# Weight splits behind the router's lists, a second last tile routed alone, and final norms without GpSimd

## The chip, the cores and the metric

The kernel runs on one core of a Trainium2 chip. A core has five engines with their own instruction queues: TensorE (PE, with weight loads as PEld), VectorE (DVE), ScalarE (ACT), GpSimd (POOL) and SyncE (SP, which issues most transfers); a queue is worked off in order, and engines wait for one another by semaphores. The metric is the device time of one launch in microseconds (us). All times below come from one profiled execution unless it is said otherwise.

## What is computed

One layer of a decoder trunk on 1024 tokens of width 1024 with 16 learned tokens ahead of them: three mixers fed by one projection, their output projected and added to the stream `h`, then a mixture of 16 experts, then a final norm. The change touches the mixture and the norm:

```python
h = h + mixed @ w_out[l]
h = h + hier_moe(rms_norm(h, norm_ffn_g[l]), router_g_w[l], router_g_b[l],
                 router_e_w[l], router_e_b[l], exp_w1[l], exp_w3[l], exp_w2[l])
return rms_norm(h, final_norm_g)[:, N_META:]
```

`hier_moe` picks for each token the best of four groups (`lg`) and in it the two best of four experts, with gates from two softmaxes; an expert is `(silu(t @ w1) * (t @ w3)) @ w2`, times its gate.

## The kernel before

**Precision.** Every large product is made of three: both factors are split into a high part (rounded) and a low part (the rest). A split of half a weight buffer (128x1024) is a copy on ScalarE (L1273) and a subtraction (L1274) on VectorE, or for some of the first weights on GpSimd. A transposed token block is split the same way when it leaves PSUM (L1201 on ScalarE, L1202 on VectorE).

**Router.** The stream is worked off in eight tiles of 128 tokens. For each, `mix` multiplies by `w_out` and adds (L867), and `logits` transposes (L878), multiplies by the router's matrix (L884), takes a root mean square (`rsqrt_mean`: two short GpSimd instructions, L271 and L273) and scales the logits (L887). The normed tile goes to DRAM (`t_d`) and the stream too (`h_d`), by SP's queue. For tile 7 the norm is a scaling on ScalarE (L893) and a product with the norm's weights on GpSimd (L894). `Router.batch(a, b)` turns the logits of tiles a to b-1 into chosen experts, counts and gates: some 40 short VectorE instructions, a few small matmuls (L1052 counts), and for each tile one-hot matrices (L1066, L1068) that PE multiplies (L1071) to lists. It is called for tiles 0 to 3, 4 and 5, and, behind the last logits, for 6 and 7. `finish` reads the lists from PSUM (L1090, L1092). The gates are written to `t_d` beside the rows (L1084).

**Experts.** `moe` is a generator: its first part, up to the first `yield`, loads three raw weights, and more is set up as the stream's tiles are done. Behind the lists, GpSimd gathers an expert's tokens from `t_d` by an indirect transfer (`gather`, L1185), block 0 always and block 1 (a second 128 tokens) only if the expert has more than 128; `come` transposes them. Then follows, in an order written by hand (`ORDER`), a round for each of 16 experts: f0 and f1 the first product of block 0 and 1, g the gate function, u and v its transpose (L1221) and split (L1227), s00, s01, s1 the second product, e00 to e11 the eviction with the token's gate (L1434 for the last three experts), t and x the next expert's transposes, a0, a1, w0, w1, b0, b1 the splits of weights two or fewer experts ahead, ga the gather. The results of the first thirteen experts are added to `h_d` by scattered transfers; for the last four the kernel gathers the rows of `h_d` into SBUF ahead (L1361), adds into them and writes the normed rows to the output (`result`, L1368).

**Final norm.** A row block of 128x1024 is squared and summed on ScalarE (L1320), its root taken by L271 and L273, and scaled by the mean and the weights: one VectorE instruction (L1330), or, for the rows that `ASIDE` names, a scaling on ScalarE (L1327) and a product on GpSimd (L1328). Rows of tokens that no late expert touches are normed in rounds 14 and 15, then those of experts 12 and 13; their steps lie in the list `later`, from which `tick(n)` takes n steps at each place of the order, n from `TICKS`.

## Time and profile before

| | |
|---|---|
| runs of the kernel | 878.46, 884.48, 885.94 us; median 884.48 |
| profiled execution | 882.01 us; span from first to last instruction 880.3 us |
| mean granted TensorE clock | 0.954 of full speed |
| busy share of the span | PE 89%, VectorE 68%, ScalarE 50%, GpSimd 31% |
| mix of tile 7 to the first expert matmul | about 563 to 595 us |
| expert loop | about 595 to 858 us |
| last norms and result writes | about 858 to 880 us |

Times are positions in the profiled execution. A row of the timeline gives start, duration, engine, line and operation, output and inputs with shapes, and how many instructions it groups (x2 means two, with one duration for both). In brackets stands how long the engine had been idle before, and what ended that: another engine's instruction, a transfer (DMA), or "issue" where the profile shows no reason. PE's own end times are modelled.

### The profile page before, as it was taken

To read this page: it belongs to the slowest core of one execution; us is meant where nothing else is said; L and a number is where in the kernel's file an instruction comes from. 1 tells how busy PE (TensorE), PEld (TensorE's weight loads), DVE (VectorE), ACT (ScalarE), POOL (GpSimd) and SP (SyncE) were. 2 spreads that over 40 slices of the span, in tenths; PEclk is the share of its full clock that TensorE was granted. 3 is DMA by queue.
4 is the path that set the end of the run, shared out by engine and by line. 5 is a ranking of instruction groups with operands and counts; after the bars stand their busy time and mean duration, and the time that the engine had idled before them with its cause. 6 is when DMAs were issued, how large, how long until landed. Compare 5 with 4: busy or idle time off the path is not lost. (4 is left out here: it accounts for less than half of the span.)

```text
span 880.3 us, 13055 instructions
## 1 busy us (share of the span) xinstructions
PE 781.9 (89%) x4402; PEld 635.6 (72%) x4403; DVE 594.7 (68%) x1292; ACT 438.4 (50%) x762; POOL 274.0 (31%) x371
## 2 busy tenths in 40 slices
PE   3999999789999989999999999827999998997880
PEld 2899998678999956555668888716788885775660
DVE  5961889977644476656534345756779677897993
ACT  7222645343323375555663231415568567686861
POOL 4499948720001000000020020341223223124374
PEclk9998999999999999999999999957999999998985
DMA  8307132031320141202232422129699979899752
GB/s 275 83 7 145 50 96 61 8 98 37 98 71 13 51 139 51 73 25 73 97 101 73 142 94 77 48 88 374 230 292 285 284 227 275 273 271 291 252 208 105
DMA packets 88987, 122.00 MB, mean 139 GB/s; under 512 B 14827, under 2 KB 69898, under 8 KB 88912
## 3 DMA queue, kind: packets, MB, share of 16 engines
q1 hardware_dynamic: 81856, 101.98, 36.2%
q0 software_dynamic: 7056, 19.09, 8.0%
q8 instruction: 39, 0.64, 0.3%
q14 instruction: 36, 0.29, 0.1%
HBM read 101.16 MB, written 26.52 MB: 145 GB/s over the span
## 5 line engine op out<-in xcount | busy, mean ns | idle before, releaser
L282 PE MATMUL psum<-arena,arena 128*128 128x512 f32 (+4 forms) x848 | 306.4, 362 | 10.9 <-DVE arena L597 7.2
L283 PE MATMUL psum<-arena,arena 128*128 128x512 f32 (+4 forms) x848 | 299.9, 354 | 0.1
L284 PE MATMUL psum<-arena,arena 128*128 128x512 f32 (+4 forms) x848 | 299.5, 354 | 0.0
L282 PEld LDWEIGHTS psum<-arena,arena 128*128 128x128 f32 x848 | 162.1, 192 | 32.1 <-DVE arena L597 8.1
L284 PEld LDWEIGHTS psum<-arena,arena 128*128 128x128 f32 x848 | 162.0, 191 | 17.0 <-DVE arena L592 0.3
L283 PEld LDWEIGHTS psum<-arena,arena 128*128 128x128 f32 x848 | 162.3, 191 | 15.4 <-issue 0.4
L1274 DVE TENSOR_TENSOR arena<-arena,arena 128x1024 fp32r<-128x1024 f32 x92 | 114.3, 1278 | 18.2 <-ACT arena L1273 16.7
L1273 ACT ACTIVATE arena<-arena 128x1024 fp32r<-128x1024 f32 x96 | 98.8, 1073 | 7.9 <-DMA arena<-in_exp_w_dram 4.7
L671 DVE CUSTOM_DVE_ANT_0 arena<-psum,arena 128x144 bf16<-128x144 f32 (+6 forms) x112 | 55.1, 506 | 46.8 <-PE psum L669 24.2
L271 POOL TENSOR_SCALAR arena<-arena 128x1 f32<-128x1 f32 (+3 forms) x35 | 13.4, 383 | 231.6 <-DVE arena L463 73.0
L729 PE MATMUL psum<-arena 128*65 128x512 f32 (+4 forms) x224 | 82.8, 455 | 0.5 <-ACT arena L726 0.5
L726 ACT ACTIVATE arena<-psum,arena 128x512 f32<-128x512 f32 (+4 forms) x112 | 59.3, 539 | 47.7 <-PE psum L723 30.8
L1238 POOL DMA_INDIRECT h_d<-arena x17 | 33.6, 1979 | 127.2 <-DVE arena L1202 64.1
L1195 PE MATMUL psum<-arena 128*128 128x128 f32 x256 | 39.7, 290 | 20.8 <-DMA arena<-t_d,arena 12.7
L1201 ACT ACTIVATE arena<-psum 128x512 fp32r<-128x512 f32 x64 | 38.6, 604 | 34.2 <-PE psum L1195 34.2
L1195 PEld LDWEIGHTS psum<-arena 128*128 128x128 f32 x256 | 31.8, 149 | 32.2 <-DVE arena L1202 9.0
L430 DVE SCALAR_TENSOR_TENSOR psum<-arena,psum 128x1024 f32<-128x1024 f32 x40 | 51.4, 1285 | 0.8
L666 PE MATMUL psum<-arena 128*128 128x144 f32 (+6 forms) x112 | 51.5, 483 | 0.0
L1202 DVE TENSOR_TENSOR arena<-psum,arena 128x512 fp32r<-128x512 f32 x64 | 43.6, 683 | 11.6 <-ACT arena L1201 11.6
L718 PE MATMUL psum<-arena 128*128 128x512 f32 (+4 forms) x112 | 47.8, 427 | 2.8 <-ACT arena L726 2.5
L440 POOL TENSOR_TENSOR arena<-arena 128x512 f32<-128x512 f32 x36 | 48.1, 1359 | 1.0 <-ACT arena L437 1.0
L437 ACT ACTIVATE arena<-arena 128x512 f32<-128x512 f32 x40 | 28.3, 720 | 35.2 <-POOL arena L440 21.0
(297 smaller groups left out, 1257.5 us busy)
## 6 DMA issues: line engine op xcount, KB each, us to landing
arena<-in_exp_w_dram SPq DMA_DIRECT2D x64, 512.0 KB
arena<-in_exp_w_dram SPq DMA_DIRECT2D x16, 1024.0 KB
arena<-in_x_dram SPq DMA_DIRECT2D x16, 512.0 KB
arena<-in_w_in_dram SPq DMA_DIRECT2D x14, 512.0 KB
arena<-cr_d SPq DMA_DIRECT2D x8, 520.0 KB
arena<-in_w_out_dram SPq DMA_DIRECT2D x8, 512.0 KB
h_d<-arena SPq DMA_DIRECT2D x8, 512.0 KB
t_d<-arena SPq DMA_DIRECT2D x8, 512.0 KB
```

The costliest lines, as they stand in the source:

```text
L282: PE.matmul(out=acc, lhsT=lh[k], rhs=rh[k], start=(k == 0), stop=False)
L283: PE.matmul(out=acc, lhsT=lh[k], rhs=rl[k], start=False, stop=False)
L284: PE.matmul(out=acc, lhsT=ll[k], rhs=rh[k], start=False, stop=(k == n - 1))
L430: V.scalar_tensor_tensor(out=yc, in0=ub[:, m, w:w + NX], scalar=cwt[:, m, w:w + 1], in1=yc, op0=OP.mult, op1=OP.add)
L440: G.tensor_tensor(out=yp[:, a:a + 512], in0=yp[:, a:a + 512], in1=o, op=OP.add)
L666: PE.matmul(out=sp, lhsT=QS[:, i * 128 - 128:i * 128], rhs=KS[:, a:b], start=True, stop=not last)
L671: V.tensor_tensor_reduce(out=jk_b()[:, :b - a], in0=sp, in1=nrow[:, a:b], scale=1.0, scalar=-3.0e38, op0=OP.add, op1=OP.max, accum_out=mp[ ...
L726: S.activation(out=pt, in_=sp, func=AF.Exp, bias=ccol[:nk, j, h:h + 1])
L729: PE.matmul(out=po[:, q0 - 512 * g:512], lhsT=vt[:nk, j, h, :], rhs=pt, start=j == 0, stop=j == last, skip_group_check=True)
L1195: PE.transpose(tp[:, k, :], xg[:, c:c + 128], ident)
L1273: S.activation(out=h[:, cs], in_=raw[:, cs], func=AF.Copy)
L1274: eng.tensor_tensor(out=l[:, cs], in0=raw[:, cs], in1=h[:, cs].bitcast(F32), op=OP.subtract)
```

## The change

Line numbers of the changed kernel are higher by some 14 in `moe` (L1274 becomes L1288, L1330 becomes L1338, L1434 becomes L1442, L1185 becomes L1199).

- `logits`: for tile 7 the GpSimd product `h2 * fg_row` comes ahead of the logits (L873) and the ScalarE scaling last (L894).
- `batch` is called for tile 6 behind `logits(6)` and for tile 7 alone behind `logits(7)`. The gates become a method of their own; for tile 7 `finish` calls it last.
- `moe`: the six half splits of the first three weights move from ahead of the lists (two weights on GpSimd, one on VectorE) to behind the first gathers, all on VectorE, each weight with its refill; three further weights are loaded ahead of the lists; two of the four token buffers are cleared later; `come(1)` stands behind the first product.
- the last norms: no row on ScalarE and GpSimd any more; the steps taken at each place are counted anew; the round behind the last expert is written out by hand, the two rows of expert 14 in one norm, those of expert 15 singly.

```diff
@@ logits
+        t = t_b()
+        if i == 7:
+            G.tensor_tensor(out=t, in0=h2[i], in1=fg_row, op=OP.mult)
...
-        t = t_b()
...
-            S.activation(out=t, in_=h2[i], func=AF.Copy, scale=r1)
-            G.tensor_tensor(out=t, in0=t, in1=fg_row, op=OP.mult)
+
+            with at_priority(400):
+                S.activation(out=t, in_=t, func=AF.Copy, scale=r1)
@@ the tiles
-        if i in (4, 5):
-            rt.batch(*{4: (0, 4), 5: (4, 6)}[i])
+        if i in (4, 5, 6):
+            rt.batch(*{4: (0, 4), 5: (4, 6), 6: (6, 7)}[i])
...
-    rt.batch(6, 8)
+    rt.batch(7, 8)
@@ Router.batch and finish
+        if b < 8:
+            self.gates(a, b)
+
+    def gates(self, a, b):
...
+        self.gates(7, 8)
@@ TICKS, ASIDE
-    "2101420301341212330033115032302",
...
+    dict(f1=1, s00=1, g0=1, x01=1, w0=1, v0=1, e01=1, x10=2, w1=1, b0=1, b1=1, x11=1),
...
-ASIDE = ((3,), (0, 2,), (0, 2,), (0,))
@@ moe
-    for t in xg_b.aps:
+    for t in xg_b.aps[:2]:
         G.memset(t, 0.0)
     raw_b.more(3)
     todo = order[3:]
+    for _ in range(3):
+        w = todo.pop(0)
+        raws[w] = load_raw(*w)
...
-    for w, eng in ((order[0], G), (order[1], V), (order[2], G)):
-        for a in range(2):
-            split(*w, a, eng, False)
     yield
     bank.use(xt=(0, 1), h=(2, 3), y=(4, 5, 6), a=(7,))
+    xgs[0, 0] = gather(slots(0, 0))
     two = nc.values_load(rt.two[0:1, 0:1], engines=[EPE, mybir.EngineType.Pool], min_val=0, max_val=(1 << NE) - 1)
-    big = nc.values_load(rt.nbl[0:1, NE:NE + 1], engines=[mybir.EngineType.Pool], min_val=0, max_val=8)
...
-            for t in raw_b.aps:
-                G.memset(t[:, 255:257], 0.0)
-            for _ in range(6):
-                refill()
+            for t in xg_b.aps[2:]:
+                G.memset(t, 0.0)
+            for w in order[:3]:
+                for a in range(2):
+                    split(*w, a, V)
+    tc.no_sync_barrier()
+    big = nc.values_load(rt.nbl[0:1, NE:NE + 1], engines=[mybir.EngineType.Pool], min_val=0, max_val=8)
...
-                if k in aside:
-                    S.activation(out=rows[k], in_=rows[k], func=AF.Copy, scale=r1[:, k:k + 1])
-                    G.tensor_tensor(out=rows[k], in0=rows[k], in1=ng_row, op=OP.mult)
-                else:
-                    V.scalar_tensor_tensor(out=rows[k], in0=rows[k], scalar=r1[:, k:k + 1],
-                                           in1=ng_row, op0=OP.mult, op1=OP.mult)
+                V.scalar_tensor_tensor(out=rows[k], in0=rows[k], scalar=r1[:, k:k + 1],
+                                       in1=ng_row, op0=OP.mult, op1=OP.mult)
...
-        for f in norm_steps(hr[NE - 1][1:]):
-            f()
-    result(NE - 1, 1)
+        tick(99)
+        e = NE - 1
+        n14 = list(norm_steps(hr[e - 1]))
+        n15 = [list(norm_steps([t])) for t in hr[e]]
...
+        do(n14[:4])
+        do_second(e, 0, 0)
+        do_second(e, 0, 1)
+        do_second(e, 1, None)
+        do_evict(e, 0, 0)
+        do_evict(e, 0, 1)
+        do(n15[0][:3])
+        do(n14[4:])
+        do_evict(e, 1, 0)
+        do_evict(e, 1, 1)
+        for b in range(2):
+            result(e - 1, b)
+        do(n15[1][:3])
+        for b in range(2):
+            do(n15[b][3:])
+            result(e, b)
```

The first place is GpSimd's queue from the last tiles' roots to the first gather. Before, it held the splits of two weights (L1274) ahead of tile 7's root (L271, L273) and the product L894 behind it:

```order
245 L1274 TENSOR_TENSOR arena_83<-arena_2795,arena_60 128x1024 x2
246 L1274 TENSOR_TENSOR arena_3625<-arena_2795,arena_60 128x1024 x2
247 L271 TENSOR_SCALAR arena_61<-arena_61 128x1
248 L273 TENSOR_TENSOR arena_61<-arena_61 128x1
249 L894 TENSOR_TENSOR arena_61<-arena_61 128x1024
250 L1286 TENSOR_LOAD arena_61
```

Now the product stands ahead of the root, and the splits are gone:

```order
244 L873 TENSOR_TENSOR arena_61<-arena_61 128x1024
245 L271 TENSOR_SCALAR arena_61<-arena_61 128x1
246 L273 TENSOR_TENSOR arena_61<-arena_61 128x1
247 L1298 TENSOR_LOAD arena_61
248 L1303 REGISTER_ALU
249 L1303 COMPARE_AND_BRANCH
250 L1199 DMA arena_61<-t_d,arena_61 128x1026
```

Only the register `two` (L1298) is loaded ahead of the gather; `big` follows three gathers later.

The second place is VectorE's queue from the end of the lists to the first corrections of gathered tokens. Before, the gate of the gathered block (L1252) and L1202 followed the lists at once:

```order
819 L1090 TENSOR_SCALAR arena_61<-psum 128x128
820 L1092 TENSOR_SCALAR arena_61<-psum 128x128 x2
821 L1291 UNCONDITIONAL_BRANCH
822 L1252 ISA arena_61<-arena_61 128x2
823 L1252 ISA arena_61 128x1
824 L1291 UNCONDITIONAL_BRANCH
825 L1252 ISA arena_61<-arena_61 128x2
826 L1252 ISA arena_61 128x1
827 L1202 TENSOR_TENSOR arena_4747<-psum,arena_4747 128x512 x3
828 L1274 TENSOR_TENSOR arena_2090<-arena_61,arena_60 128x1024 x2
```

Now six splits (L1288) lie between the lists (L1102, L1104) and the first two L1216, which were L1202:

```order
843 L1102 TENSOR_SCALAR arena_61<-psum 128x128
844 L1104 TENSOR_SCALAR arena_61<-psum 128x128 x2
845 L1303 UNCONDITIONAL_BRANCH
846 L1288 TENSOR_TENSOR arena_83<-arena_2795,arena_60 128x1024 x2
847 L1303 UNCONDITIONAL_BRANCH
848 L1288 TENSOR_TENSOR arena_2091<-arena_61,arena_60 128x1024 x2
849 L1288 TENSOR_TENSOR arena_3625<-arena_2795,arena_60 128x1024 x2
850 L1216 TENSOR_TENSOR arena_4789<-psum,arena_4789 128x512 x2
```

The third place is VectorE's queue from the last split to the end. Before: evictions (L1434) of blocks (14,0) and (14,1) around the last split, the turned gate L1227, two norm rows (L1330), then all four evictions of expert 15 and the last three rows:

```order
1185 L1434 SCALAR_TENSOR_TENSOR arena_61<-psum,arena_61 128x512 x2
1186 L1274 TENSOR_TENSOR arena_3625<-arena_61,arena_60 128x1024
...
1189 L1434 SCALAR_TENSOR_TENSOR arena_61<-psum,arena_61 128x512 x2
1190 L1227 SCALAR_TENSOR_TENSOR arena_2606<-psum,arena_2606 128x256
...
1192 L1330 SCALAR_TENSOR_TENSOR arena_2795<-arena_2795,arena_61 128x1024
1193 L1330 SCALAR_TENSOR_TENSOR arena_61<-arena_61 128x1024
...
1195 L1434 SCALAR_TENSOR_TENSOR arena_61<-psum,arena_61 128x512 x2
...
1198 L1434 SCALAR_TENSOR_TENSOR arena_61<-psum,arena_61 128x512 x2
...
1200 L1330 SCALAR_TENSOR_TENSOR arena_61<-arena_61 128x1024 x2
...
1202 L1330 SCALAR_TENSOR_TENSOR arena_61<-arena_61 128x1024
```

Now (L1338 is the norm row, L1442 the eviction, L1241 the turned gate):

```order
1221 L1288 TENSOR_TENSOR arena_3625<-arena_61,arena_60 128x1024
...
1224 L1338 SCALAR_TENSOR_TENSOR arena_2795<-arena_2795,arena_61 128x1024 x2
1225 L1338 SCALAR_TENSOR_TENSOR arena_61<-arena_61 128x1024
1226 L1442 SCALAR_TENSOR_TENSOR arena_61<-psum,arena_61 128x512
1227 L1338 SCALAR_TENSOR_TENSOR arena_61<-arena_61 128x1024
1228 L1442 SCALAR_TENSOR_TENSOR arena_61<-psum,arena_61 128x512
1229 L1241 SCALAR_TENSOR_TENSOR arena_2606<-psum,arena_2606 128x256
...
1233 L1442 SCALAR_TENSOR_TENSOR arena_61<-psum,arena_61 128x512 x2
1234 L1338 SCALAR_TENSOR_TENSOR arena_61<-arena_61 128x1024 x2
1235 L1442 SCALAR_TENSOR_TENSOR arena_61<-psum,arena_61 128x512 x2
...
1237 L1338 SCALAR_TENSOR_TENSOR arena_61<-arena_61 128x1024
...
1240 L1338 SCALAR_TENSOR_TENSOR arena_61<-arena_61 128x1024
```

All four rows of experts 12 and 13 stand on VectorE, three of them ahead of the first eviction of (14,1), all ahead of the turned gate, and one row alone is left behind each of the last steps.

## Rows read from the trace of the kernel before

**Rows 1.** By stretch: from:to, us, busy PE PEld DVE ACT POOL, PEclk, DMA share, GB/s
```profile
590.00:606.00 16.00, 10.42 (x44) 8.38 (x44) 4.51 (x7) 5.04 (x8) 3.32 (x10) 0.74 0.95 332
612.00:805.00 193.00, 182.35 (x876) 145.18 (x874) 153.85 (x260) 132.45 (x209) 55.73 (x34) 0.98 0.88 269
830.00:858.00 28.00, 24.20 (x88) 18.50 (x86) 27.93 (x31) 19.11 (x31) 20.08 (x12) 0.82 0.56 204
858.00:881.00 23.00, 0.00 (x0) 0.00 (x0) 7.52 (x6) 3.34 (x5) 11.18 (x11) 0.57 0.25 101
```
**Rows 2.** Timeline of VectorE from tile 7's mix to the lists
```profile
564.79 6.48 DVE L1274 TENSOR_TENSOR arena<-arena,arena 128x1024 fp32r<-128x1024 f32 x2 [0.76 <-PE psum L283]
...
576.73 0.24 DVE L887 SCALAR_TENSOR_TENSOR arena<-psum,arena 128x20 f32<-128x20 f32 x1 [3.22 <-POOL arena L273]
...
577.99 2.41 DVE L1035 SCALAR_TENSOR_TENSOR arena<-arena 128x16 f32<-128x16 f32 x2
...
587.00 0.48 DVE L1092 TENSOR_SCALAR arena<-psum 128x128 f32<-128x128 f32 x2
```
**Rows 3.** Timeline of GpSimd, same stretch and the first gather
```profile
564.48 11.31 POOL L1274 TENSOR_TENSOR arena<-arena,arena 128x1024 fp32r<-128x1024 f32 x4 [5.81 <-ACT arena L1273]
...
577.95 2.34 POOL L894 TENSOR_TENSOR arena<-arena 128x1024 f32<-128x1024 f32 x1 [1.26 <-ACT arena L893]
588.78 1.29 POOL L1185 DMA_INDIRECT arena<-t_d,arena  x1 [8.48 <-issue]
```
**Rows 4.** Timeline of TensorE from tile 7's transposes to the second expert
```profile
572.08 0.66 PE L878 MATMUL psum<-arena 128*128 128x128 f32 x4 [2.78 <-DVE arena L867]
...
582.69 0.19 PE L1052 MATMUL psum<-arena 128*128 128x32 bf16 x1 [8.14 <-DVE arena L998]
...
593.48 1.97 PE L1195 MATMUL psum<-arena 128*128 128x128 f32 x8 [6.72 <-DMA arena<-t_d,arena]
595.28 0.79 PE L282 MATMUL psum<-arena,arena 128*128 128x512 f32 x1
...
606.75 0.66 PE L1195 MATMUL psum<-arena 128*128 128x128 f32 x4 [2.86 <-DVE arena L1202]
...
611.50 0.78 PE L282 MATMUL psum<-arena,arena 128*128 128x512 f32 x1
```
**Rows 5.** Timeline in the loop: gathers alone and beside splits
```profile
609.60 2.03 POOL L1185 DMA_INDIRECT arena<-t_d,arena  x1 [12.90 <-DVE arena L1214]
...
616.03 2.35 DVE L1274 TENSOR_TENSOR arena<-arena,arena 128x1024 fp32r<-128x1024 f32 x2
616.52 1.59 POOL L1185 DMA_INDIRECT arena<-t_d,arena  x1 [4.90 <-DVE arena L1227]
...
656.67 1.02 POOL L1185 DMA_INDIRECT arena<-t_d,arena  x1 [0.30 <-issue]
```
**Rows 6.** Timeline of VectorE in the tail
```profile
828.49 4.29 DVE L1330 SCALAR_TENSOR_TENSOR arena<-arena 128x1024 f32<-128x1024 f32 x2
...
840.06 4.62 DVE L1330 SCALAR_TENSOR_TENSOR arena<-arena 128x1024 f32<-128x1024 f32 x2
...
845.38 2.61 DVE L1274 TENSOR_TENSOR arena<-arena,arena 128x1024 fp32r<-128x1024 f32 x1
...
852.35 1.27 DVE L1330 SCALAR_TENSOR_TENSOR arena<-arena,arena 128x1024 f32<-128x1024 f32 x1
853.54 3.42 DVE L1330 SCALAR_TENSOR_TENSOR arena<-arena 128x1024 f32<-128x1024 f32 x1
856.88 1.40 DVE L1434 SCALAR_TENSOR_TENSOR arena<-psum,arena 128x512 f32<-128x512 f32 x2
```
**Rows 7.** Timeline of GpSimd in the tail
```profile
850.91 1.01 POOL L273 TENSOR_TENSOR arena<-arena 128x4 f32<-128x4 f32 x1
...
873.16 1.05 POOL L1368 DMA_INDIRECT out_dram<-arena  x1 [1.61 <-DVE arena L1330]
```
**Rows 8.** Timeline of ScalarE in the tail
```profile
858.36 1.06 ACT L1320 ACTIVATE arena<-arena 128x1024 bf16<-128x1024 f32 x1 [2.00 <-issue]
```

## What it will do

> **What bounds the kernel now.** I read first the busy times by stretch, then what each engine waited for at the two ends of the expert loop, where the change lies. From 612 to 805 us the loop is bound by TensorE: 182.35 busy us of 193 [rows 1]. The change leaves the order of that stretch as it is, so a start moved by x moves its end by x. Ahead of it, PE waits: 8.14 us before the list matmul L1052, 6.72 us for the first gather before L1195, and the first expert matmul starts at 595.28 [rows 4]. This is a serial chain: logits of tile 7, router, lists, gather, transposes. Behind it the binding engine changes. From 830 to 858 VectorE is busy 27.93 of 28 us, PE 24.20; from 858 to 881 PE does nothing, and norms and result writes run alone [rows 1]. Only microseconds in these two chains count.
>
> One effect stands in both. A VectorE instruction with two SBUF sources does not proceed while GpSimd runs a 128x1024 product. A pair of splits (L1274) takes 2.35 us alone [rows 5] and 6.48 beside GpSimd's splits; two L1035 of 16 columns take 2.41 us, beginning with GpSimd's L894 and ending with it [rows 2, 3]. A norm row (L1330) takes 1.27 us, or 3.42 beside a product [rows 6]. The page "SBUF — State Buffer" of the Trainium skill, section "SBUF: two separate sides", calls this an exclusive lock on a port pair that VectorE and GpSimd share, held for a whole instruction; these rows agree.
>
> **The router, step by step.** (1) The splits of the first weights leave the place before the lists: on GpSimd 11.31 us ahead of tile 7's rsqrt [rows 3], on VectorE 6.48 us [rows 2] ahead of its last mix addition. PE's L878 stood idle 2.78 us for that addition [rows 4]; I take 2.4 off, which ends it at about 569.6. (2) GpSimd's product of tile 7 (2.34 us [rows 3]) now follows that addition, 569.6 to 572.0, ahead of the rsqrt; it holds VectorE's two-source work on tile 6's lists until 572.0. That work then needs about 4 us (two tiles' took 3.6 from 576.73 to 582.69 [rows 2, 4] without the stall of L1035, and the one-hots of one tile come on top), so L887 of tile 7 comes at 576.0 instead of 576.73 [rows 2]. (3) From L887 to PE's L1052 it was 5.96 us (576.73 to 582.69 [rows 2, 4]). The stall of L1035 goes (2.41 less two at 0.15: 2.1) and one tile needs fewer instructions (0.5): 3.4, so L1052 at 579.4. (4) From there to the end of the lists it was 4.8 us (587.00 + 0.48 [rows 2]). Four of eight one-hot instructions go, each worth 0.26; what was moved behind them, the gates of tile 7, is partly between them: 3.6, so 583.0. (5) The gather followed 1.3 us later (588.78 [rows 3]), behind two register loads, now one: 584.0.
>
> What the change puts in its way: six splits on VectorE behind the lists, 583.3 to 590.3 at 2.35 a pair [rows 5]; their copies on ACT (a square of that size there takes 1.06 [rows 8]) keep pace. x00's correction L1202 is queued behind them, and PE's first matmul waits for it. A gather's issue took 1.02 us alone and 2.03 beside splits [rows 5]: 1.0 later. Tile 7's row write and gates wait in SP's queue behind three weight loads of 1.5 MB; those can start at about 573 (they need tile 7's transposes done) and at 332 GB/s [rows 1] take 4.7 us, over before 583. Another 1 MB load waits only for the row write and shares the DMA engines with the gather; I add 0.5, with 0 and 3.2 (the whole MB first) as ends. The gather took 4.7 us to PE's L1195 (588.78 to 593.48) and PE 1.8 more to 595.28 [rows 3, 4]: 584.0 + 1.0 + 0.5 + 4.7 + 1.8 = 592.0, and VectorE is free at 590.3. Gain 3.3, between 0 (the whole MB, gates late by 1) and 5.
>
> From there to the next expert it was 16.2 us (595.28 to 611.50 [rows 4]), with 2.86 us [rows 4] in which L1202 stood behind two splits of a late weight. Three further weights now load before the lists, so that wait goes; but the second block of transposes (`come(1)`) stands behind the matmuls, sixteen transposes through two banks, some 2 us more. I take 0.7, between -1 and 3. **Router: -4.0 (1 to -8).**
>
> **The tail.** Six norm rows leave ACT and GpSimd and become VectorE instructions. Removed: the holds of 1.8, 2.1, 1.4 and 2.1 us between 828 and 857 (4.29 and 4.62 for pairs that take 2.5 alone, 2.61 for a split of 1.2, 3.42 for a row of 1.27 [rows 6]): 7.4. Added by then: five rows at a spacing of 1.19 (852.35 to 853.54 [rows 6]): 6.0. So VectorE gains little; the order does the rest, and not all of it for good. Write (15,1) for the second block of expert 15. In the last round four muls of experts 12 and 13 stand ahead of and between the evictions of block (14,1) and the turned gate of (15,1). Their rsqrt ended at 851.9 [rows 7], about 851.0 without ACT's copies; VectorE comes to them at 851.6. Three muls and an eviction end at 855.9, which is when PE gets the bank for the second half of (15,0); another mul, an eviction and L1227 end at 858.2, which is when PE may begin (15,1). Twelve matmuls, first at half clock, end at about 862 (before: 857.7). Meanwhile the norm of expert 14 runs: square of its last row 1.06 [rows 8] from 857.9, rsqrt 1.0 [rows 7], and behind two evictions, which end at 859.6, two muls: 862.4 at the latest. Then two evictions 1.4 [rows 6]: 863.8; square 1.06: 864.9; rsqrt 0.85 (a single value; 1.01 for four [rows 7]); mul 1.27: 867.0; issue at 867.3. Before, the last issue came at 873.16 [rows 7], 13.6 us behind the last eviction, since a three-row norm, a GpSimd product and four issues lay between; now 3.5. **Tail: -5.9.** Bounds: -9 if PE isn't held, -2.5 if (15,1) stays at half clock and GpSimd's rsqrt waits behind two issues.
>
> The dropped empty yields only move norm steps by a place; the later memsets (two at about 1 us on an idle GpSimd) and the later `big` load stand behind the gathers: nothing, and if they hold GpSimd it is the second gather, not needed before `come(1)`.
>
> **Sum.** Profiled execution 882.01 us (span 880.3): 882.0 - 4.0 - 5.9 = 872.1. That execution lies 2.5 below the median of the runs, 884.48, and inside their 878.46 to 885.94; I keep 872 as the forecast.
>
> **Rivals.**
> A. As worked out, 866 to 876. Chance 0.62.
> B. The gather is held by the splits. It needs GpSimd's access to SBUF while VectorE issues six two-source instructions without a gap. Against: 2.03 us is the longest gather issue of the loop, and another beside a pair of splits took 1.59 [rows 5], so GpSimd gets in after one. For: never six in a row in this trace. If all six go first: 7 us in place of 1, f0 at 598, total 878. Chance 0.12. The same section of "SBUF — State Buffer" has this as a trap: descriptors written by GpSimd starve while VectorE holds the pair. That rule speaks against the change; by it the gather waits at least for the running split. Rows 5 show a wait of that size, not of several.
> C. The tail gives nothing, because VectorE's added rows hold PE: if PE, held by the four muls, stays at half clock, (15,1) ends at 865 and the last issue is at 870.4; with the last rsqrt behind two issues on GpSimd (1.05 each [rows 7]) it is at 872.5. The tail gives 2.8 to 0.7, the total is 875 to 877 with the router at -4.0. For: VectorE is full there [rows 1]. Against: the 7.4 us of holds. Chance 0.12.
> D. Slower. The six splits run at the held price. It takes a GpSimd instruction beside each; at 3.2 us (half of 6.48 [rows 2]) they end at 602.5, f0 comes at 603.3, 8 late, and with the tail at -5.9 and no gain behind f0 the total is 884. It decides from 2.9 us a split. Against: GpSimd has only gathers and two memsets there, no product. Chance 0.06.
> E. Better, below 866: the second expert's start gains 3 and PE isn't held in the tail. Chance 0.08.
>
> **How the numbers follow.** The likeliest case gives 872. For eight in ten the range must hold A and most of B and C: 864 to 880. About 1% (8.8 us) is what a measurement of this kernel can tell from no change. Against the median that is 875.6: most of A and all of E lie below it, B, C, D and A's end above: faster 0.6, same 0.35, slower 0.05 (D with a lost tail).
>
> **What would show it.** Right: L867 of tile 7 near 569; no L1035 above 0.3 us; L1052 near 579; the first gather issued near 584, f0 near 592; the norm rows at 1.27 throughout, (15,1) ending near 862 and the last issue 3 to 4 us behind the last eviction. Wrong: a gather issue above 2 us or f0 behind 595 (B, D); PE idle for L1227 of (15,1) and a last matmul behind 864 (C); or a loop longer than its 193 us, from loads that come in another order.

## The result

The changed kernel takes 875.96 us (median of 20 runs, 872.15 to 882.21) against 881.48 for the kernel before on the same chip (20 runs, 877.17 to 885.94): ratio 0.9941, interval 0.9922 to 0.9959. That is 5.2 us less (6.9 to 3.6), inside the range given and about half of the 9.9 us that the likeliest case gave. The interval leaves out 1, so the kernel is faster, but by less than the 1% that the prediction set for a change. The profiled execution has a span of 875.3 us (880.3 before).

Absolute times of two executions can't be set side by side here. Two executions of the same program, that of before, reach the mix addition of tile 6's second half at 554.72 and 557.70 us, though the code ahead of it is one and the same. So every stage below is counted from an event of its own execution. First the stretches of the changed kernel, as from:to, us, busy PE, PEld, DVE, ACT, POOL, granted clock of PE, DMA share, GB/s:

```profile
585.00:600.00 15.00, 2.06 (x9) 1.83 (x10) 7.25 (x8) 1.70 (x4) 5.89 (x5) 0.50 0.78 285
607.00:800.00 193.00, 181.41 (x878) 145.09 (x877) 156.54 (x269) 134.85 (x214) 53.53 (x31) 0.97 0.85 258
830.00:853.00 23.00, 17.64 (x75) 13.60 (x74) 22.17 (x30) 16.38 (x30) 9.13 (x9) 0.95 0.71 267
853.00:876.00 23.00, 6.90 (x21) 4.63 (x19) 13.01 (x15) 3.45 (x6) 10.22 (x11) 0.72 0.26 101
```

In the loop PE is about as busy as it was (181.41 us of 193, where [rows 1] has 182.35). The last 23 us now hold PE work and 13.01 us of VectorE, where before PE did nothing [rows 1]. In the 15 us ahead of the first expert PE works 2.06 us, while the DMA engines are 0.78 busy: PE waits with much data moving, which is the first thing to follow up.

The table shows each stage in one profiled execution of each kernel. The columns up to f0 are us after the start of tile 6's last mix addition, the one of its second half: the last mix addition of tile 7 (L867 before, L864 in the changed kernel), the end of the lists, the issue of the first gather. "Landing" is from that issue to PE's first transpose, f0 is the first expert matmul. "e1" is from f0 to the gate transposes of the second expert, "e1 to e13" from there to those of the fourteenth, "last" from there to the last gate transpose, "PE end" from it to the last L282 matmul (L279 in kernels with the new tail; the last matmul of all ends 0.9 us later), "issue" from that to the last result issue, "rest" from there to the end. Experiments stand in it too; each is told below.

```
                 add   lists gather landing f0    | e1    e1-e13 last  PE end issue rest
before          16.63  32.75 34.06  4.70    40.56 | 31.96 183.27 38.14  8.22  16.29 7.17
before_again    16.60  32.75 34.04  4.71    40.55 | 29.75 182.16 38.07  8.33  16.17 7.17
the change      14.12  27.46 31.12  9.12    42.04 | 30.27 184.14 34.41 12.87   7.52 6.40
after_again     14.12  27.57 31.14  8.16    41.10 | 31.21 184.27 34.41 12.88   7.52 6.39
tail_only       16.63  32.76 34.06  4.78    40.65 | 28.22 183.18 34.53 13.71   6.59 6.73
tail_again      16.63  32.76 34.06  4.71    40.57 | 29.75 180.78 35.31 14.14   6.38 6.73
router_only     14.12  27.70 32.41  8.40    42.60 | 30.52 183.84 38.07  7.85  16.51 6.83
writes_on_act   14.12  27.45 30.13  7.71    39.65 | 30.14 183.92 34.42 12.89   7.52 6.39
refill_hold     14.12  27.62 32.23  5.41    39.44 | 30.48 183.80 34.44 11.62   8.78 6.39
all_hold        14.12  27.47 27.38  4.55    33.73 | 32.32 183.83 34.43 11.64   9.63 6.39
act_and_hold    14.12  27.45 29.43  4.79    36.02 | 30.22 183.50 34.42 12.90   7.50 6.41
both_again      14.12  27.47 30.51  4.68    36.99 | 32.33 183.81 34.46 13.68   6.73 6.41
router_mended   14.12  27.47 29.97  5.30    37.07 | 31.78 183.74 38.16  8.14  16.11 6.82
muls_behind     14.12  27.48 30.85  5.62    38.28 | 31.41 183.37 34.43  8.91  11.42 6.40
```

Two things stand out. The lists come 5.3 us earlier (27.46 against 32.75), and yet the first expert begins 1.5 us later (42.04 against 40.56). The tail gains in every piece but one: 3.7 in the last two rounds, 8.8 between PE's end and the last issue, 0.8 behind it, less 4.65 by which PE ends later: 8.6 in all.

From tile 6's last mix addition to the end the columns sum to 325.6 and 322.2 us in the two traces of the kernel before, 317.7 and 317.8 in those of the change, and 313.6 and 313.7 in those of its tail alone (tail_only, tail_again).

**The router in the changed kernel.** VectorE's timeline (start, us, line, operation, out<-in, count, idle before it and its releaser):

```profile
571.82 0.69 DVE L864 TENSOR_TENSOR arena<-psum,arena 128x512 f32<-128x512 f32 x1
...
572.63 2.39 DVE L1013 SCALAR_TENSOR_TENSOR arena<-arena 128x16 f32<-128x16 f32 x1
...
579.19 0.18 DVE L1035 SCALAR_TENSOR_TENSOR arena<-arena 128x16 f32<-128x16 f32 x1
...
584.68 0.48 DVE L1104 TENSOR_SCALAR arena<-psum 128x128 f32<-128x128 f32 x2
585.08 6.89 DVE L1288 TENSOR_TENSOR arena<-arena,arena 128x1024 fp32r<-128x1024 f32 x6
```

The stall on L1035 [rows 2] is gone (0.18), and has moved to L1013 of tile 6's lists: 2.39 us for 16 columns, as long as GpSimd's product beside it. The six splits take 6.89 us, 1.15 each, so nothing holds them. GpSimd's timeline of the same stretch:

```profile
572.59 2.39 POOL L873 TENSOR_TENSOR arena<-arena 128x1024 f32<-128x1024 f32 x1 [12.10 <-DVE arena L1025]
...
588.82 2.03 POOL L1199 DMA_INDIRECT arena<-t_d,arena  x1 [12.43 <-DVE arena L1288]
```

GpSimd is idle for 12.43 us ahead of the gather, and the lists it needs were there at 585.2. L1288 named as releaser is the running split and no source of the gather; what the gather does read is t_d, the tokens with their gates, written by DMA. So SP's queue comes next (start, us for issuing, line, out<-in, count):

```profile
577.07 1.49 SPq L1158 DMA_DIRECT2D arena<-in_exp_w_dram  x3
578.64 0.45 SPq L895 DMA_DIRECT2D t_d<-arena  x1
581.33 0.34 SPq L1096 DMA_DIRECT2D t_d<-arena  x1
587.74 0.38 SPq L1162 DMA_DIRECT2D arena<-in_exp_w_dram  x1
588.21 0.97 SPq L1158 DMA_DIRECT2D arena<-in_exp_w_dram  x2
589.73 0.37 SPq L1162 DMA_DIRECT2D arena<-in_exp_w_dram  x1
```

Tile 7's gates, a write of about 1 KB, are issued at 581.33 behind three weight loads of 512 KB (577.07) and the 512 KB row write (578.64). The view of that line's DMAs gives their times to landing:

```profile
DMA to landing us min/median/max: 3.2/5.9/6.6
```

6.6 us is the last one: it lands at 587.9, and the gather is issued at 588.82. From 585.2 to 587.7 the DMA engines are nearly idle (share 0.02), so in the last 2.7 us of the 6.6 no bulk data moved. Then 3 MB of further weight loads start between 587.74 and 589.73, beside the gather's own transfer: 1 MB (587.74) is the last of the three weights taken ahead of the lists, and 2 MB are refills that the splits set free. PE's timeline:

```profile
572.57 0.66 PE L878 MATMUL psum<-arena 128*128 128x128 f32 x4 [0.35 <-DVE arena L864]
...
575.90 0.17 PE L1052 MATMUL psum<-arena 128*128 128x16 bf16 x1 [1.86 <-DVE arena L998]
...
575.95 1.05 PE L884 MATMUL psum<-arena 128*128 128x20 f32 x8
...
581.29 0.17 PE L1052 MATMUL psum<-arena 128*128 128x16 bf16 x1 [2.75 <-DVE arena L998]
...
597.94 1.97 PE L1209 MATMUL psum<-arena 128*128 128x128 f32 x8 [13.50 <-DMA arena<-in_exp_w_dram]
...
599.74 0.79 PE L279 MATMUL psum<-arena,arena 128*128 128x512 f32 x1
...
605.86 0.39 PE L281 MATMUL psum<-arena,arena 128*128 128x512 f32 x1
...
614.58 0.48 PE L279 MATMUL psum<-arena,arena 128*128 128x512 f32 x1
```

L878 no longer waits (0.35 where [rows 4] had 2.78). The second half of tile 7's logits, L884, stands in PE's queue behind tile 6's count L1052, which waits 1.86 us for VectorE, which was held by the product. So L884 begins at 575.95, and what needs tile 7's transposed rows to be read comes after it: the weight loads that take their place are issued at 577.07. The first transpose starts 9.12 us behind the gather's issue; before it was 4.70 [rows 3, 4]. The last two rows are the last matmul of the first expert's first product and the first of the second expert's.

**The tail in the changed kernel.** VectorE:

```profile
851.90 2.48 DVE L1338 SCALAR_TENSOR_TENSOR arena<-arena,arena 128x1024 f32<-128x1024 f32 x2
...
855.49 0.74 DVE L1442 SCALAR_TENSOR_TENSOR arena<-psum,arena 128x512 f32<-128x512 f32 x1
856.15 1.27 DVE L1338 SCALAR_TENSOR_TENSOR arena<-arena 128x1024 f32<-128x1024 f32 x1
857.34 0.74 DVE L1442 SCALAR_TENSOR_TENSOR arena<-psum,arena 128x512 f32<-128x512 f32 x1
858.00 0.41 DVE L1241 SCALAR_TENSOR_TENSOR arena<-psum,arena 128x256 fp32r<-128x256 f32 x1
...
860.43 2.48 DVE L1338 SCALAR_TENSOR_TENSOR arena<-arena 128x1024 f32<-128x1024 f32 x2 [0.70 <-POOL arena L273]
862.83 1.40 DVE L1442 SCALAR_TENSOR_TENSOR arena<-psum,arena 128x512 f32<-128x512 f32 x2
...
866.44 1.28 DVE L1338 SCALAR_TENSOR_TENSOR arena<-arena 128x1024 f32<-128x1024 f32 x1 [1.01 <-POOL arena L273]
```

Every norm row (L1338) takes 1.27 or 1.28 us; the holds of [rows 6] are gone. Four of them stand ahead of and between the evictions L1442 of block (14,1). PE pays for that:

```profile
856.29 0.50 PE L279 MATMUL psum<-arena,arena 128*128 128x512 f32 x1 [2.39 <-DVE arena L1442]
...
861.89 0.40 PE L281 MATMUL psum<-arena,arena 128*128 128x512 f32 x1
```

GpSimd's last instructions are rsqrts of single values and issues:

```profile
861.85 1.47 POOL L273 TENSOR_TENSOR arena<-arena 128x1 f32<-128x1 f32 x1
...
866.64 2.01 POOL L1376 DMA_INDIRECT out_dram<-arena  x1 [0.23 <-issue]
868.95 0.96 POOL L1376 DMA_INDIRECT out_dram<-arena  x1 [0.30 <-POOLq L1545]
```

The last issue starts 4.7 us behind the last eviction's end (864.23), where before it was 13.6.

### The profile page after: what moved, and what is told of

Read it like the earlier page. It is cut to its first block, busy times and chain, and to the rows that moved or that the text cites. A ratio compares the mean times of both kernels' runs of the same rounds, so it can differ in the third digit from the quotient of the medians.

```text
span 875.3 us, 13059 instructions
## 1 busy us (share of the span) xinstructions
PE 780.7 (89%) x4404; PEld 635.8 (73%) x4405; DVE 595.6 (68%) x1322; ACT 431.3 (49%) x758; POOL 248.6 (28%) x357
## 5 line engine op out<-in xcount | busy, mean ns | idle before, releaser
L279 PE MATMUL psum<-arena,arena 128*128 128x512 f32 (+4 forms) x848 | 306.4, 362 | 13.4 <-DVE arena L594 5.9
L279 PEld LDWEIGHTS psum<-arena,arena 128*128 128x128 f32 x848 | 163.3, 193 | 34.3 <-DVE arena L594 6.5
L1288 DVE TENSOR_TENSOR arena<-arena,arena 128x1024 fp32r<-128x1024 f32 x96 | 113.5, 1219 | 13.8 <-ACT arena L1287 13.0
L271 POOL TENSOR_SCALAR arena<-arena 128x1 f32<-128x1 f32 (+2 forms) x36 | 12.7, 352 | 244.3 <-DVE arena L460 73.1
L1252 POOL DMA_INDIRECT h_d<-arena x17 | 34.6, 2037 | 127.7 <-DVE arena L1216 64.2
L1216 DVE TENSOR_TENSOR arena<-psum,arena 128x512 fp32r<-128x512 f32 x64 | 43.6, 683 | 19.4 <-ACT arena L1215 19.4
```

The source lines that it names most:

```text
L279: PE.matmul(out=acc, lhsT=lh[k], rhs=rh[k], start=(k == 0), stop=False)
L1288: eng.tensor_tensor(out=l[:, cs], in0=raw[:, cs], in1=h[:, cs].bitcast(F32), op=OP.subtract)
```

## The experiments

**The two parts apart.** The theory after the result: the tail works, and the router's gain is lost between the lists and the first expert, so the tail alone should be faster than the change. The rival: the tail's gain is overestimated, and the router gives some of it.

tail_only leaves the router as before and takes over the norms, the ticks and the end by hand:

```
-    for _ in range(7 if W == 1 else 10):
-        yield lambda: None
-ASIDE = ((3,), (0, 2,), (0, 2,), (0,))
+TICKS = (dict(f1=1, s00=1, ...
...
+        n14 = list(norm_steps(hr[e - 1]))
+        n15 = [list(norm_steps([t])) for t in hr[e]]
```

> Only the part on the last norms is changed; the router, the splits and the loads stay as in the kernel before. Theory (the tail gave what was forecast and more, the start of the loop took some of it back): the first expert matmul stays at about 595.3 us, the second round before the last no longer waits (2 us), and the last issue comes about 6.5 us nearer to the first matmul of expert 15: 8 to 9 us less than the kernel before in all, 3 less than the changed kernel. Rival (the tail's gain comes from the late start, which lets transfers run ahead): 5 us less or no more than the changed kernel.

router_only is the other half: splits behind the lists, batches (6, 7) and (7, 8), gates at the end, three loads ahead, with the old norms:

```
-        if i in (4, 5):
-            rt.batch(*{4: (0, 4), 5: (4, 6)}[i])
+        if i in (4, 5, 6):
+            rt.batch(*{4: (0, 4), 5: (4, 6), 6: (6, 7)}[i])
...
-    rt.batch(6, 8)
+    rt.batch(7, 8)
```

> Only the part on the router, the splits and the early loads is changed; the last norms stay as in the kernel before. Theory: the first expert matmul comes at about 599.7 us, 4.5 later than before, the loop gets back about 1.4 of it at the second expert, and the end is 2 to 4 us later than the kernel before. As the prediction had it: 4 us earlier.

Measured: tail_only 871.57 us beside 884.44 of before, ratio 0.9874 (0.9843 to 0.9905), 11.1 us less. router_only 883.1, ratio 1.0003 (0.9974 to 1.0031). So the router gives none of the gain, though it costs nothing clear of noise either, where 2 to 4 us had been expected. The change's 0.9941 lies above the tail's interval, but in another comparison; the two never ran side by side, and the 4 us between them are those of the sums above. The stages say where the router's gain goes: router_only starts the first expert 2.0 us later than before though its lists are 5.1 us earlier.

**What keeps the gather.** Two suspects from SP's queue: the gates' write behind 2 MB on one queue (three loads and the row write), and the 3 MB that start beside the gather. Each is taken away by itself.

writes_on_act issues tile 7's two writes from ScalarE's queue:

```
-        SY.dma_start(out=t_d[i * 128:i * 128 + 128, 0:D], in_=t)
+        (SY if i < 7 else S).dma_start(out=t_d[...], in_=t)
...
-        self.nc.sync.dma_start(out=self.t_d[a * 128:b * 128, D:D + 2]...
+        (self.nc.sync if b < 8 else S).dma_start(out=self.t_d[a * 128:b * 128, D:D + 2]...
```

> The changed kernel, but tile 7's row and its gates are written through ScalarE's queue instead of SyncE's, where 1.5 MB of weight loads stand ahead of them. Theory (the first gather waits for the gates, which wait in that queue): the gates land 2 to 3 us behind their issue instead of 6.6, the gather is issued at about 585.5 instead of 588.8, the first expert matmul comes about 3 us earlier, and the whole is 2 to 3 us shorter than the changed kernel. Rival (the DMA engines are simply full, whatever the queue): the gates still land 5 us or more behind their issue, and no time is gained. Rival (the splits on VectorE hold GpSimd): the gather is issued no earlier than 588.

refill_hold keeps the refills of the six splits back until the first gather has landed, by a small transfer on SP that reads the gathered block:

```
-                    split(*w, a, V)
+                    split(*w, a, V, False)
...
+    hold = A.alloc("hold", [2])
     with tc.manual_schedule():
+        SY.dma_start(out=hold, in_=xgs[0, 0][:, D:D + 2])
+        for _ in range(3):
+            refill()
         come(0)
```

> The changed kernel, but the three weight loads that the six splits set free wait in SyncE's queue until the first gather has landed. Theory (the gather shares the DMA engines with 3 MB of loads): the gather is still issued at about 588.8, but lands 5 to 6 us behind that instead of 9.1, and the first expert matmul comes 3 to 4 us earlier, at about 596; the whole is 2 to 4 us shorter than the changed kernel if the later weights are not missed. Rival (the gather is slow because GpSimd writes its descriptors beside the splits): it lands 9 us behind its issue as before.

Measured: writes_on_act 874.84, ratio 0.9907 (0.9877 to 0.9938); refill_hold 871.9, ratio 0.9873 (0.9843 to 0.9904), beside the same runs of before (884.44). In the stages each mends mostly its own piece: with the writes on ScalarE's queue the gather is issued at 30.13 in place of 31.12, a third of the 3 us expected, and still takes 7.71 to land (9.12 and 8.16 in the two traces of the change); with the refills held it is issued as late as ever (32.23), and lands in 5.41. The timeline of refill_hold, SP, GpSimd and PE:

```profile
587.76 0.38 SPq L1162 DMA_DIRECT2D arena<-in_exp_w_dram  x1
...
588.85 2.23 POOL L1199 DMA_INDIRECT arena<-t_d,arena  x1 [13.54 <-DVE arena L1288]
...
594.25 1.97 PE L1209 MATMUL psum<-arena 128*128 128x128 f32 x8 [10.74 <-DMA arena<-t_d,arena]
```

The issue takes 2.23 us beside the splits, with one load of 1 MB running, the last of the three weights ahead of the lists (587.76). In muls_behind below it takes 2.32 with the DMA engines nearly idle (share 0.07), so a slow issue does not need the loads; it fits the 1 us that was forecast for the splits. The two refills held back, 2 MB, are what held the transfer.

**Both together, and with the loads ahead away too.** act_and_hold is writes_on_act and refill_hold in one. all_hold leaves the writes on SP and moves the three weights that were loaded ahead of the lists (3 MB) behind the hold as well:

```
-    for _ in range(3):
-        w = todo.pop(0)
-        raws[w] = load_raw(*w)
...
         SY.dma_start(out=hold, in_=xgs[0, 0][:, D:D + 2])
+        for _ in range(3):
+            w = todo.pop(0)
+            raws[w] = load_raw(*w)
         for _ in range(3):
             refill()
```

> Both single remedies at once: tile 7's row and gates written through ScalarE's queue, and the three refills held until the first gather has landed; the three loads ahead of the lists stay. Theory (two separate causes): gather issued 2 us earlier and landing 3 us sooner than in the changed kernel, first expert matmul 36.5 to 38 us behind tile 6's mix (40.6 before, 42.0 in the changed kernel, 39.4 to 39.7 with either remedy alone). Rival (one cause in two guises, the loads' bytes have to pass anyway): about 39.5 as with one remedy.

> The changed kernel, but all six weight loads (three that it issues ahead of the lists, three that the splits set free) wait in SyncE's queue until the first gather has landed. Theory (the lists come 5 us earlier, and all of that is lost to tile 7's writes queued behind loads, 2.9 us, and to loads beside the gather, 4.4 us): the gates land within 2.5 us of their issue, the gather is issued 1 to 2 us behind the lists and lands about 5 us later, the first expert matmul comes 5 us nearer to tile 6's mix than in the kernel before (35 to 36 us instead of 40.6), and the whole is 4 to 6 us shorter than the changed kernel. Rival (the weights of the second expert then come late): the first matmul is early, but the second expert's gives it back, and the whole is no better than with the three refills held.

Two controls ran with them, the change once more and a second trace of the kernel before (the "third expert" of that text is the second in the table above):

> The changed kernel once more, beside the others on the same chip. Measured so far: the changed kernel at 0.9941 of the kernel before, the tail part alone at 0.987, the router part alone at 1.000. If the two parts add up, the changed kernel must come out at 0.987 here, and 0.9941 was its chip or its executions; if they hinder each other, it stays at 0.994. In its first trace PE waited 2.4 us longer for a gather in the middle of the loop (at 748 us) than in any other trace: if the parts hinder each other, that wait is there again.

> The kernel before once more, for a second trace. The tail part alone has the same instructions in the same order as the kernel before up to the round of expert 14, and yet its trace was 3.8 us shorter between the first and the third expert. If that is a matter of the execution, this trace shows a distance between the first expert matmul and the gate transposes of the third expert of 28 to 32 us, other than 32.0; if it is the program, 32.0 again.

Measured beside 881.16 of before: act_and_hold 871.11, ratio 0.9898 (0.9851 to 0.9945); all_hold 871.06, 0.9891 (0.9844 to 0.9938); after_again 875.82, 0.9946 (0.9915 to 0.9978), which repeats the result; before_again 881.58. Its "e1" is 29.75 where the trace of before had 31.96, so that distance is a matter of the execution. The wait named for after_again is there again:

```profile
745.92 1.94 PE L1209 MATMUL psum<-arena 128*128 128x128 f32 x8 [3.69 <-DMA arena<-t_d,arena]
```

In the first trace of the change it was 3.93 us. It was at most 2.76 in every other trace, and 2.43 in writes_on_act, which has both parts too; so the two parts together do not suffice for it. The timeline of act_and_hold:

```profile
577.75 0.33 ACTq L1096 DMA_DIRECT2D t_d<-arena  x1
583.56 1.45 POOL L1199 DMA_INDIRECT arena<-t_d,arena  x1 [10.75 <-DMA arena<-in_exp_w_dram]
...
588.35 1.97 PE L1209 MATMUL psum<-arena 128*128 128x128 f32 x8 [7.49 <-DMA arena<-t_d,arena]
```

and of all_hold:

```profile
583.83 1.29 POOL L1196 DMA_INDIRECT arena<-t_d,arena  x1 [8.69 <-DVE arena L1102]
...
588.38 1.97 PE L1206 MATMUL psum<-arena 128*128 128x128 f32 x8 [5.18 <-DMA arena<-t_d,arena]
```

In act_and_hold the gather's issue comes 5.8 us behind that of the gates, with four of the six splits (581.49 to 588.38) still to come, and takes 1.45, so rival B, all six splits first, is out. The landing is 4.79 behind it. In all_hold no load runs from 575 until the gather has landed: GpSimd's releaser is now the list itself (L1102), the gather is issued at 27.38, when the lists end, and lands in 4.55. Both suspects are shown and they add. The larger part of the delay of tile 7's writes goes with the traffic: with ScalarE's queue the gather was issued at 29.4 to 30.9 in five executions, with SP's at 31.1 to 32.4 in four, and without the loads at 27.4. How much of it the splits add is not shown, since in all_hold the gather is issued just ahead of the first of them, and the landing of the writes on ScalarE's queue is not in the traces. The first expert starts 6.8 us earlier than before in all_hold and 4.5 in act_and_hold.

**Does an earlier start arrive at the end?** all_hold and act_and_hold are no faster than tail_only was in its comparison, though their first expert starts 4 to 7 us earlier. So the tail alone, the mended router alone and both were run side by side, tail_again and both_again being tail_only and act_and_hold unchanged, router_mended being router_only with the two edits of act_and_hold (three refills are held, not the six of the expectation).

> The tail of the change alone, a second time, so that it stands beside the mended kernels on one chip. From the single profiles the tail is worth 8.5 us in the last rounds (third last gate transposes to the last 3.6, PE's end later by 4.65, last issue nearer by 8.8, end 0.8). If the parts add, this kernel must be slower than both_again by the 4.5 us by which the first expert starts earlier there (0.990 against 0.985). If an earlier start of the first expert is given back in the loop, the two are the same within 0.3%.

> The whole change with the row write and gates of tile 7 on ACT's queue and the six refills held until the first gather has landed. First expert 36 us behind tile 6's mix addition (before 40.6, the change 41 to 42). If the parts add: 0.985, 4 us faster than the tail alone. If the start is given back in the loop: 0.99, the same as the tail alone.

> The router of the change with both mendings and the old tail. If an earlier start of the first expert arrives at the end: 4 to 5 us faster than before, ratio 0.995. If the loop gives it back: 1.000, as the router of the change without the mendings.

Measured beside 881.85 of before: tail_again 875.22, ratio 0.9915 (0.9885 to 0.9946); both_again 870.99, 0.9872 (0.9844 to 0.99); router_mended 879.3, 0.9979 (0.995 to 1.0008). Side by side, the mended router takes 4.2 us from the tail alone (6 runs each, and their intervals overlap) and 1.9 (by the interval between 4.4 less and 0.7 more) from before. The tail alone is 11.1 us faster than before in one comparison and 7.5 in the other, and its stages give 7 to 8. The runs don't settle whether the mended router's 3.5 to 4.5 us arrive whole. Nor do the traces: from tile 6's last mix addition to the end the two executions of act_and_hold took 311.0 and 314.4 us, all_hold 312.0, refill_hold 315.0 and the tail alone 313.6 and 313.7, so two executions of one program differ by about as much as the gain that is looked for. The stages suggest that a part is given back behind f0: "e1" is 28.2, 29.8, 29.8 and 32.0 in the four executions with the old router, and 30.1 to 32.3 in the ten with the new one; "e1 to e13" is 180.8 to 183.3 against 183.4 to 184.3.

The granted clock is where "e1" differs: it is 28.2 to 29.8 in the three executions in which the clock stays up at the second expert, and 30.1 to 32.3 in the eleven in which it falls. The windows below stand at 8 us behind f0 and on (columns as in the first fence), before_again first:

```profile
606.26:610.26 4.00, 1.39 (x10) 0.82 (x8) 3.72 (x5) 2.45 (x6) 0.00 (x0) 1.00 1.07 381
610.26:614.26 4.00, 1.80 (x13) 1.36 (x14) 3.93 (x10) 4.00 (x7) 1.86 (x1) 1.00 1.05 391
614.26:618.26 4.00, 4.00 (x20) 3.27 (x19) 4.00 (x5) 4.00 (x6) 0.17 (x1) 1.00 1.07 373
```

and the changed kernel:

```profile
607.74:611.74 4.00, 2.17 (x14) 1.46 (x14) 3.90 (x9) 3.59 (x7) 0.00 (x0) 1.00 0.07 17
611.74:615.74 4.00, 2.16 (x12) 1.53 (x11) 3.97 (x9) 3.81 (x6) 2.02 (x1) 0.90 0.83 260
615.74:619.74 4.00, 4.00 (x14) 3.17 (x13) 4.00 (x8) 2.54 (x4) 0.00 (x0) 0.67 0.81 246
```

In before_again the clock stays at 1.00, the upper of TensorE's two levels (2.4 GHz). In the changed kernel it falls, and the second expert's first 24 matmuls take 7.20 us (614.58 to 621.78) in place of 5.63 (614.15 to 619.78). The clock falls at this place in all ten executions with the new router, and in one of the four with the old (before, e1 of 31.96). In the 8 us up to the second expert's first matmul PE was busy for 3.71 in the changed kernel and for 3.19 in before_again, so more work there did not keep the clock up. The stretch between the first expert's first product and the second expert's, in which PE has only transposes, does differ. In before_again it goes from 606.55 to 614.15, 7.60 us:

```profile
606.16 0.39 PE L284 MATMUL psum<-arena,arena 128*128 128x512 f32 x1
...
614.15 0.48 PE L282 MATMUL psum<-arena,arena 128*128 128x512 f32 x1
```

In the changed kernel it goes from 606.25 to 614.58, 8.33 us, since the second block's transposes (`come(1)`) now stand behind that product and not among its matmuls. In each of the eleven executions with a fall it is longer than in any of the three without. No run changed this stretch alone, so that it brings the fall is not shown. Nor was a cause found for the 1 us or so in "e1 to e13"; in the two traces of the change a part of it stands in the wait for a gather shown above.

**The four multiplications ahead of block (14,1).** muls_behind is act_and_hold with these four behind the evictions and the turned gate, and nothing else moved:

```
-         t11=2, w1=1, u1=1, b0=1, b1=1, end=4),
+         t11=2, end=8),
```

> both_again with the four multiplications of experts 12 and 13 behind the evictions of block (14,1) and the turned gate of (15,1), no longer between them: the only difference. PE then begins the second half of (15,0) 3.6 us earlier and the last gate transposes to the last matmul take about 9 us in place of 12.9. If PE sets the end of the tail: 3 us faster than both_again. If VectorE does, which has 0.7 us idle from PE's hold to its last multiplication: at most 1 us.

Measured 870.86, ratio 0.9874 (0.984 to 0.9908), against 870.99 of both_again beside it. Timeline of VectorE from the evictions on:

```profile
843.99 1.41 DVE L1442 SCALAR_TENSOR_TENSOR arena<-psum,arena 128x512 f32<-128x512 f32 x2
...
852.47 2.48 DVE L1338 SCALAR_TENSOR_TENSOR arena<-arena 128x1024 f32<-128x1024 f32 x2 [0.64 <-POOL arena L273]
854.87 1.41 DVE L1442 SCALAR_TENSOR_TENSOR arena<-psum,arena 128x512 f32<-128x512 f32 x2
```

PE is no longer held: from the last gate transpose to the last matmul it is 8.91 us instead of 12.9 to 13.7. But the evictions of (15,1) come no earlier, since the same rows stand ahead of them on VectorE, and the stretch from PE's end to the last issue, 6.7 to 7.5 us in the two executions of act_and_hold, grows to 11.42. The sum is 20.3 us against 20.4. So PE, which the changed order holds for 4 us, costs nothing there: VectorE, with 0.64 us idle in the 11 up to the last evictions, sets the end.

## Why the forecast was half right

**Router, up to the lists: right, and a little better.** L878 waits 0.35 us and the last mix addition comes 2.5 us earlier (2.4 forecast). The product holds VectorE as worked out, on L1013. L1035's stall is gone. Tile 7's L1052 comes 4.4 us earlier (3.3 forecast), the end of the lists 5.3 (4.5 forecast).

**From the lists to the first expert: wrong, in two terms.** The forecast was a gain of 3.3 us for f0, the change lost 1.5 (0.5 and 2.0 in two other executions of that router). First, "Tile 7's row write and gates wait in SP's queue behind three weight loads of 1.5 MB; those can start at about 573 ... over before 583", priced at nothing. The loads were issued at 577.07, which is 574.1 in the time of the trace of before (this execution is 2.98 us behind it there). The gates followed at 581.33 and took 6.6 us to land. So the gather was issued 3.7 us behind the lists in place of the 1.0 of the sum: 2.7 late. The step had counted when the loads would be over, which was right (the DMA engines fell idle at 585.2, 582.2 in the time of before), and no time for the write itself, nor for 512 KB of row write ahead of it. all_hold shows this term by taking it away; act_and_hold takes away a part. Second, "I add 0.5" for the load beside the gather. From issue to the first transpose it took 9.12 us where the sum had 6.2; it was 2.9 late here, and 2.0 to 2.2 in the two others. Not one load of 1 MB ran beside the gather but 3 MB: the 2 MB of refills that the splits set free were not in the sum. refill_hold takes these away, leaves the 1 MB, and lands in 5.41, inside the 6.2 of the sum: the load that was counted was not underpriced, the others were left out. The two terms, 5.6 us, less the 0.8 by which the lists were better, are the 4.8 between the forecast and the run. The upper end kept for the second, 3.2, did contain it; the first had no end above 1 us, and so the router's range (0 to 5 for f0) did not hold what came.

**To the second expert.** The first matmul of the second expert comes 14.84 us behind f0 (599.74 to 614.58) where before had 16.22: 1.4 gained, 0.7 forecast. What wasn't foreseen is that these matmuls then run partly at the lower clock (1.2 GHz), which costs 1.6, and which the trace of before had too. Up to the second expert's gate transposes the change gains 1.7 on that trace and loses 0.5 on before_again.

**Tail: right in its mechanism, too small.** PE's end is 4.65 us later from the last gate transpose (4.3 forecast for (15,1)), the rows all take 1.27 or 1.28, and the last issue starts 4.7 us behind the last eviction (3.5 forecast, 13.6 before): the last two issues stand in a row, 866.64 for 2.01 and 868.95. The mis-sized term is the one for the rounds ahead: 7.4 us of holds against 6.0 of added rows, "so VectorE gains little". PE reached the last gate transposes 3.7 us earlier. The holds [rows 6] stood in rounds in which PE waited for VectorE; that most of the added rows came to stand where VectorE had room, or behind, is the likely reason, and no run tests it alone. Up to the last issue the tail gained 7.8 (5.9 forecast), and another 0.8 behind it, for which there was no term.

**The rivals.** B fell: the gather's issue took 2.03 us beginning beside the fourth of six splits, and 1.45 in act_and_hold, beginning beside the second, so the splits did not hold it to their end. The trap in the Trainium skill ("SBUF — State Buffer", section "SBUF: two separate sides") did not show beyond the running split, as [rows 5] had it. That section states the trap for VectorE instructions in a 2-port perf mode; no run here shows whether the splits are such. The sign named for B and D, "f0 behind 595", did come (599.74, or 596.8 in the time of before), but from neither: the splits ran at 1.15 us. C fell, and muls_behind shows why its premise was wrong: PE's hold is not on the path. In number the result is A's upper end, but not by A's route: the router gave nothing and the tail more than worked out. That the total came out at 876 and not at 880 is owed to the tail, so the range was met by two misses that pull opposite ways, which is luck.

**Queues and loads.** Tile 7's writes got through sooner on a queue without bulk loads, but not freely: with ScalarE's queue the gather was issued 29.4 to 30.9 us after the mix addition, with SP's 31.1 to 32.4, and 27.4 without the loads. So the larger share went with the loads themselves, whatever the queue. The Trainium skill, "DMA: Bandwidth & Descriptors", section "Queues, rings and completion order", says that a DMA engine goes round between the queues that have work for it, packet by packet. From that one would expect a gain on a queue of its own; the traces agree with a gain of 0.2 to 3 us, and it was not the whole delay.

**What is best now.** The change with the two writes on ScalarE's queue and the refills held is at 0.9898 and 0.9872 of before in two comparisons, with the multiplications behind at 0.9874, and all_hold is at 0.9891. act_and_hold and all_hold are each about 4.7 us faster than the change beside them. Against the tail alone (0.9874 and 0.9915) the first is 4.2 us faster in the one comparison that has both, and refill_hold (0.9873) no faster in the other.

## What to carry to other kernels

When a short chain that ends in a gather or a small write is pulled forward, the weight loads behind it are pulled forward too: list every transfer that becomes ready in that window, on every queue, and price the chain's own small writes and gathers by rows that show them beside loads, not alone. Bulk loads can be held back with a tiny transfer that depends on the gather, where the loop has time for them later; here that brought the gather's landing from 8 or 9 us to about 5. In a tail, ask which engine has no idle time left: here, taking a hold of 4 us off PE changed nothing, because VectorE was full.

## What the runs showed of the hardware

- A write of about 1 KB took 6.6 us to land behind 1.5 MB of loads and a 512 KB write on the same queue (the changed kernel); the fastest write from the same line landed in 3.2.
- An indirect gather of 128 rows took 4.6 to 5.6 us from issue to PE's first use where the refills were held back, and 7.7 to 9.1 beside 3 MB of loads. Its issue on GpSimd took 1.29 us in the trace of before, and 1.45 to 2.32 when it began amid a run of six two-source VectorE instructions; these took 1.15 each in the changed kernel.
- TensorE's granted clock fell at the start of the second expert in all ten executions with the new router and in one of four with the old. In the changed kernel that cost 1.6 us, though PE had been busier ahead of it (3.71 of 8 us) than in an execution in which the clock stayed up (3.19).
- The same instructions ahead of the router ended up to 4.5 us apart in executions of different kernels (553.2 to 557.7 us), and 3 us apart in two executions of one kernel. Stages counted from an event of the same execution agreed to 0.3 us up to the end of the lists.
